# Written lists for the vector work of an up-projection, and earlier reads on the way down

## The chip, the cores and the metric

The kernel runs on one core of one Trainium2 chip. Five engines of the core matter: TensorE (PE, its weight loads shown as PEld), VectorE (DVE), ScalarE (ACT), GpSimd (POOL) and SyncE (SP), which here issues all DMA transfers. Each takes its instructions from a queue of its own, in the order in which the program left them there. The metric is the time of one execution on the device, in microseconds, as the median of the runs shown.

## The reference

One inference step of a two-layer decoder: 1024 tokens of a prompt and 8 x 4 tokens of a sample group share the weights. Each layer has a recurrent mixer, cross attention and a feed-forward part. The change touches the last one:

```python
def conv_ffn(h, w_up, conv_w, conv_b, w_down, prev):
    up = h @ w_up                                   # 1024 -> 2 x 2816
    ext = jnp.concatenate([prev, up], axis=1)
    c = conv_b + conv_w[0] * ext[:, 0:L]
    for j in range(1, CONV_W):                      # CONV_W = 3, causal
        c = c + conv_w[j] * ext[:, j:j + L]
    a, b = jnp.split(c, 2, axis=-1)
    return (silu(a) * b) @ w_down, ext[:, L:]
```

## The kernel before

Every product in float32 is made of three matmuls, `mm3`: both operands are split into a high part (a cast on ScalarE) and a low part (a subtraction on VectorE), and high x high, high x low and low x high are added in a bank of PSUM.

**Units of the up-projection.** `ffn` works through 22 columns f of 128 features, each for both halves (a and b) of `w_up`. Column 0 is done plainly. Each further one, f = 1 to 21, is a *unit*, a product of two 2 x 2 block matrices in the seven products of a Strassen scheme (`products`, L866). A unit has 14 *steps*: products 1, 2, 6, 5, 7, 3, 4 in this order, each for two halves c of 264 columns; a step is 12 matmuls. What a step leaves in its bank is taken by `ffn_take` (L1114) into the tiles `ext`: products 1, 6 and 5 (steps 0, 1, 4, 5, 6, 7) by a copy on ScalarE (L1123), products 2, 7 and 3 (steps 2, 3, 8 to 11) by an add on VectorE (L1127) and a multiplication on GpSimd (L1128), product 4 (steps 12, 13) by a multiplication on VectorE (L1125). Product 6 goes on in the bank of product 1, so step 4 can begin only when the copy of step 0 is done; in the same way steps 8 and 9 follow the copies of steps 4 and 5, steps 10 and 11 those of 6 and 7, and step 12 the add of step 8.

**Weights of the next unit.** `Blocks.steps` (L229) prepares them during the present unit: four sums and differences of 512 columns on GpSimd (L237, L238, L239, L243), and for four sets a cast on ScalarE (L223) and a low part on VectorE (L224). In the trace the sets are `whi`/`wlo` (product 1 and 2), `wh1`/`wl1` (products 5 and 4), `whs`/`wls` (6 and 7, tiles of the same tag) and `w4u` (product 3). Three buffers `wraw` take the raw weights.

**Convolution of the unit before.** `ffn_conv` (L1147) puts its work on the list `slow`: for each half h of the tokens, `first` (two activations, L1169), four `more` (L1172), a silu (L1176) and products (L1186, L1189) that are stored in DRAM; and on GpSimd sums of stored rows (L1199, L1204). `tick` takes items from `slow` as an estimate of free time allows.

**Order.** The tile framework draws the order of every engine's queue: it goes through the program with a model of the instructions' durations and takes from what is ready. So the queues need not have the program's order, and what the model thinks ready may not be so on the chip. `copied` ties the `w4u` parts behind the last copy of `ffn_take`.

**The way down.** `Down.run` (L416) multiplies the stored rows with `w_down` in the same scheme: seven products of six blocks i of 4, 3 and 3 row tiles (48 or 36 matmuls). `load` reads a weight block, `other` a second one where the product takes a sum of two, `sums` adds them on GpSimd, `parts` splits the result (L347), `fetch` reads stored rows y, `join` (L366) subtracts two of them on GpSimd, and `split` (L380) makes their high and low parts.

Of the kernel before, what the change touches and what calls it, by code (L numbers as in the profile page):

```python
# [18 lines left out]
P = 128  # L19
# [4 lines left out]
NS = 8  # L24
# [28 lines left out]
CUTS = ((0, 4), (4, 3), (7, 3))  # L53
OH = 3
# [154 lines left out]
class Blocks:  # L209


    def __init__(self, k, name, srcs, n):
        self.k, self.name, self.srcs, self.n, self.w = k, name, srcs, n, n * P
        self.raw, self.f = [None, None], {}
# [14 lines left out]
    def steps(self, at):  # L229
# [3 lines left out]
        for s in at:  # L233
# [54 lines left out]
class Down:  # L288
# [127 lines left out]
    def run(self):  # L416
# [3 lines left out]
        for i, (p, mp, j) in enumerate(self.at):  # L420
# [8 lines left out]
            for c in range(2):  # L429
# [24 lines left out]
class Kernel:  # L454
    def __init__(self, tc, ins, outs):
# [7 lines left out]
        self.copied = None  # L463
# [52 lines left out]
    def run(self, gen):  # L516
        return Task(gen).finish()

# [347 lines left out]
    def products(self, weights, acts, n, name, take):  # L866
# [4 lines left out]
        for s, (p, c) in enumerate(ORDER):  # L871
# [9 lines left out]
            self.tick(us - take(p, c, ps))  # L881
# [75 lines left out]
    def ffn(self, l, norm, ahead, cuts=None, post=None):  # L957
# [43 lines left out]
        self.ffn_conv(l, 0, exts)  # L1001
        for u, f in enumerate(range(1, NFT)):
            if f % 4 == 1 and f + 3 < NFT:
                state = Task(self.conv_state(l, f + 3))
            exts = self.ffn_ext(l, f)
            for s in self.products(todo[u], acts, 4, f"u{l}_{f}", self.ffn_take(exts, rstd)):
                self.ahead(todo, u, s)
# [12 lines left out]
            self.ffn_conv(l, f, exts)  # L1020
# [126 lines left out]
    def ffn_conv(self, l, f, exts):  # L1147
# [6 lines left out]

        pair, odd = f // 2, f % 2

# [3 lines left out]
        def half(h):  # L1160
            o, w = h * H, (H, CW - H)[h]
            ct = []
            wv = lambda j, q: self.cw[:, j, f + q * NFT:f + q * NFT + 1]

            def first():
                t = self.c(f"ct{l}{f}{h}")
                ct.extend([t[:, (CW - H) * q:(CW - H) * q + w] for q in range(2)] + [t])
                for q in range(2):
                    nc.scalar.activation(out=ct[q], in_=exts[q][0][:, o:o + w], func=AF.Identity, scale=wv(0, q), bias=wv(3, q))  # L1169

            def more(j, q):
                nc.vector.scalar_tensor_tensor(out=ct[q], in0=exts[q][0][:, o + j:o + j + w], scalar=wv(j, q), in1=ct[q], op0=ALU.mult, op1=ALU.add)  # L1172
# [1272 lines left out]
```

## Time and profile before

| | |
|---|---|
| median of three runs | 3252.09 us (3251.09 to 3258.42) |
| the profiled execution, its span | 3257.31 us, 3255.5 us |
| PE, PEld | busy 3110.3 us (96%), 2958.9 us (91%) |
| VectorE, ScalarE, GpSimd | 72%, 43%, 42% busy |
| the chain that ended last | PE 53%, VectorE 24%, GpSimd 12% of the span |
| DMA | 37.5% of 16 engines, mean 123 GB/s |

Busy times are shares of the whole span; a stage can look quite different. A matmul's end is modelled, and matmuls overlap. The chain is followed back from the last instruction to what released each one.

### The profile page before, as it was taken

Reading aid. Unit: us, or ns where it says so; the run is one execution under the profiler, and the core shown is the slowest. Engines: PE = TensorE matmul, PEld = TensorE weight load, DVE = VectorE, ACT = ScalarE, POOL = GpSimd, SP = SyncE. Lnnn points to the kernel's source line nnn. Section 1 sums busy time; section 2 is a strip of 40 time slices with the busy share of each in tenths; the row PEclk is TensorE's granted clock in tenths of the full one; section 3 lists DMA queues with packets and bytes.
Section 4 is the critical chain, followed back from the end, with each engine's and each line's share of the span. In section 5 each row is a group of like instructions: output and inputs, shape, how many; then the busy total and the mean of one; then the engine's idle time right before and its main releaser. Section 6 shows DMA issues by size and latency. Waiting matters only on the chain.

```text
span 3255.5 us, 64230 instructions
## 1 busy us (share of the span) xinstructions
PE 3110.3 (96%) x25741; PEld 2958.9 (91%) x25741; DVE 2329.9 (72%) x4274; ACT 1405.4 (43%) x2788; POOL 1358.7 (42%) x1494
## 2 busy tenths in 40 slices
PE   8999899999989999999999999999999899999988
PEld 6998888998889999999999999889989899999988
DVE  6649967834798787779864444675379977877896
ACT  7222255444464444453342334244446444444424
POOL 4011113300457777736621111240035777774482
PEclk9999999999999999999999999999999999999999
DMA  8513264345122222267531121225422222225853
GB/s 259 193 47 97 82 205 158 106 143 186 44 87 94 87 81 91 94 234 256 184 112 53 45 58 57 81 64 178 147 94 95 82 94 88 79 93 198 282 181 106
DMA packets 391349, 400.05 MB, mean 123 GB/s; under 512 B 26157, under 2 KB 314076, under 8 KB 391052
## 3 DMA queue, kind: packets, MB, share of 16 engines
q1 hardware_dynamic: 391052, 395.97, 37.5%
q8 instruction: 202, 3.31, 0.4%
q14 instruction: 95, 0.78, 0.1%
HBM read 303.84 MB, written 92.05 MB: 122 GB/s over the span
## 4 chain that ended last, share of the span: by engine, by line
PE 53%; DVE 24%; POOL 12%; issue 6%; ACT 3%; DMA 2%; SPq 0%; DVEq 0%; POOLq 0%; ACTq 0%
DVE ct L1172 6%; POOL ext L1128 5%; PE bd L765 3%; PE bd L763 3%; PE bd L764 3%; PE pjxq L764 2%; PE pjxq L763 2%; PE pjxq L765 2%; DVE ct L1186 1%; POOL wru L243 1%; DVE ext L1127 1%; PE blu L763 1%; PE blu L765 1%; ACT ct L1169 1%; PE blu L764 1%
## 5 line engine op out<-in xcount | busy, mean ns | idle before, releaser
L1128 POOL TENSOR_TENSOR ext<-ext,rstdff 128x264 f32<-128x264 f32 (+2 forms) x336 | 327.1, 998 | 187.4 <-DVE ext L1127 186.3
L1172 DVE SCALAR_TENSOR_TENSOR ct<-ext,cw,ct 128x528 f32<-128x528 f32 (+1 forms) x352 | 350.6, 1033 | 65.9 <-ACT ct L1169 65.7
L1169 ACT ACTIVATE ct<-ext,cw 128x544 f32<-128x544 f32 (+1 forms) x176 | 141.1, 831 | 167.8 <-POOL ext L1128 104.4
L763 PE MATMUL blu<-hhff,whiu 128*128 128x264 f32 x672 | 191.6, 286 | 0.0
L765 PE MATMUL blu<-hhff,wlou 128*128 128x264 f32 x672 | 190.8, 285 | 0.0
L892 POOL TENSOR_TENSOR o<-o 128x528 f32<-128x528 f32 x4 | 5.4, 1338 | 359.7 <-DVE xo0bb L273 179.9
L1123 ACT COPY ext<-blu 128x264 f32<-128x264 f32 (+2 forms) x336 | 98.3, 324 | 95.3 <-PE blu L765 95.2
L763 PEld LDWEIGHTS blu<-hhff,whiu 128*128 128x128 f32 x672 | 127.5, 190 | 0.0
L765 PEld LDWEIGHTS blu<-hhff,wlou 128*128 128x128 f32 x672 | 127.2, 189 | 0.0
L764 PE MATMUL pjxq<-hlxa,whxq 128*128 128x352 f32 x384 | 126.3, 329 | 0.0
L763 PE MATMUL pjxq<-hhxa,whxq 128*128 128x352 f32 x384 | 126.2, 329 | 0.0
L765 PE MATMUL pjxq<-hhxa,wlxq 128*128 128x352 f32 x384 | 124.9, 325 | 0.0
L347 DVE TENSOR_TENSOR wlod<-wrd,whid 128x768 fp32r<-128x768 f32 (+1 forms) x60 | 83.3, 1389 | 54.5 <-ACT whid L347 54.5
L347 ACT CAST whid<-wrd 128x768 fp32r<-128x768 f32 (+1 forms) x60 | 54.5, 909 | 151.5 <-PE bd L764 91.4
L1127 DVE TENSOR_TENSOR ext<-ext,blu 128x264 f32<-128x264 f32 (+2 forms) x336 | 107.5, 351 | 0.0
L224 DVE TENSOR_TENSOR w4u<-wru,w4u 128x512 fp32r<-128x512 f32 x42 | 30.3, 721 | 103.9 <-ACT w4u L223 103.9
L763 PE MATMUL blu<-hhff,w4u 128*128 128x264 f32 x336 | 95.8, 285 | 1.1 <-ACT ext L1123 1.1
L764 PE MATMUL blu<-hhff,whiu 128*128 128x264 f32 x336 | 96.7, 288 | 0.0
L764 PE MATMUL blu<-hlff,w4u 128*128 128x264 f32 x336 | 95.6, 285 | 0.0
L765 PE MATMUL blu<-hhff,w4u 128*128 128x264 f32 x336 | 95.5, 284 | 0.0
L764 PE MATMUL blu<-hlff,whiu 128*128 128x264 f32 x336 | 95.5, 284 | 0.0
L1176 ACT ACTIVATE ct<-ct 128x528 f32<-128x528 f32 x88 | 57.4, 652 | 70.7 <-DVE ct L1172 70.7
(2290 smaller groups left out, 12980.4 us busy)
## 6 DMA issues: line engine op xcount, KB each, us to landing
wru<-in_ffn_w_up SPq DMA_DIRECT2D x88, 512.0 KB
wrd<-in_ffn_w_down SPq DMA_DIRECT2D x56, 384.0 KB
bdb<-ct SPq DMA_DIRECT2D x80, 264.0 KB
wrkv<-in_xa_w_kv SPq DMA_DIRECT2D x32, 512.0 KB
kc<-in_cache_mem_k SPq DMA_DIRECT2D x64, 256.0 KB
vc<-in_cache_mem_v SPq DMA_DIRECT2D x64, 256.0 KB
wrd<-in_ffn_w_down SPq DMA_DIRECT2D x28, 512.0 KB
bdt<-ct SPq DMA_DIRECT2D x40, 264.0 KB
```

The source lines that it names most:

```text
L243: gt(out=a[:, w:], in0=a[:, w:], in1=self.s[:, :w], op=ALU.subtract)
L347: self.cast = nc.scalar.copy(out=hi, in_=src), nc.vector.tensor_tensor(out=lo, in0=src, in1=hi, op=ALU.subtract)
L763: nc.tensor.matmul(ps, wh, ah, start=first, stop=False, **kw)
L764: nc.tensor.matmul(ps, wh, al, start=False, stop=False, **kw)
L765: nc.tensor.matmul(ps, wl, ah, start=False, stop=last, **kw)
L1123: self.copied = nc.scalar.copy(out=d, in_=z)
L1127: nc.vector.tensor_tensor(out=d, in0=d, in1=z, op=ALU.add)
L1128: nc.gpsimd.tensor_tensor(out=d, in0=d, in1=r, op=ALU.mult)
L1169: nc.scalar.activation(out=ct[q], in_=exts[q][0][:, o:o + w], func=AF.Identity, scale=wv(0, q), bias=wv(3, q))
L1172: nc.vector.scalar_tensor_tensor(out=ct[q], in0=exts[q][0][:, o + j:o + j + w], scalar=wv(j, q), in1=ct[q], op0=ALU.mult, op1=ALU.add)
L1176: nc.scalar.activation(out=a, in_=a, func=AF.Silu)
L1186: nc.vector.tensor_tensor(out=d[:, :n], in0=a[:, :n], in1=b[:, :n], op=ALU.mult)
```

## The change

The work that `slow` and `Blocks.steps` held during units is cut into named pieces. `UNIT` lists for each step which pieces are issued after the step's bank is taken: `c` is a piece of the convolution of the column before, `w` a piece of the next unit's weights (`d1` to `d4` the differences, `h` a cast, `l` a low part), `s` a sum of rows. From the second unit on, `strict` ties every instruction of these pieces and of `ffn_take`, `ffn_ext` and `ffn_conv` on VectorE, ScalarE and GpSimd to the one before it on its engine, so each queue has the written order. The second raw block of the next but one unit is loaded at step 7, not 13, and the tie `copied` is gone. On the way down rows y are fetched two blocks ahead, not one, and second weight blocks three ahead, not four (six still, from the second product on to the third).

```diff
+ENGINES = (mybir.EngineType.DVE, mybir.EngineType.Activation, mybir.EngineType.Pool)
+UNIT = {0: ("c first 0 1", "c more 0 1 0", "s"), 1: ("c more 0 1 1", "w d3"), 2: ("c more 0 2 0", "w d1"), 3: ("c more 0 2 1", "w d2", "w ha"),
+        4: ("c silu 0", "w la"), 5: ("w h1", "c product 0"), 6: ("w l1", "c first 1 0", "w d4"), 7: ("c first 1 1", "c more 1 1 0"), 8: ("c more 1 1 1",),
+        9: ("c more 1 2 0",), 10: ("w hs", "c more 1 2 1"), 11: ("c silu 1", "w ls"), 12: ("c product 1", "w h4"), 13: ("w l4",)}
 OH = 3
...
@@ -248,10 +254,39 @@
                 self.parts(b, ("s1", "a22"), k.c(f"wh1{n}", F32R)[:, :2 * w], k.c(f"wl1{n}", F32R)[:, :2 * w])
             elif s == 12:
                 t = k.c(f"w4{n}", F32R)
-                with ExitStack() as ctx:
-                    if k.copied is not None:
-                        ctx.enter_context(k.tc.issue_after(k.copied.ins))
-                    self.parts(a[:, w:], ("s4",), t[:, :w], t[:, w:2 * w])
+                self.parts(a[:, w:], ("s4",), t[:, :w], t[:, w:2 * w])
+
+    def piece(self, q):
+
+        k, w, n, nc = self.k, self.w, self.name, self.k.nc
+        gt = nc.gpsimd.tensor_tensor
+        a, b = self.raw
+        if q == "d3":
+            self.s = k.c(f"ws{n}")[:, :2 * w]
+            gt(out=self.s[:, w:], in0=a[:, :w], in1=b[:, :w], op=ALU.subtract)
+        elif q == "d1":
+            gt(out=b[:, :w], in0=b[:, :w], in1=b[:, w:], op=ALU.add)
+        elif q == "d2":
+            gt(out=self.s[:, :w], in0=b[:, :w], in1=a[:, :w], op=ALU.subtract)
+        elif q == "d4":
+            gt(out=a[:, w:], in0=a[:, w:], in1=self.s[:, :w], op=ALU.subtract)
+        elif q[0] == "h":
+            names = {"a": ("a11", "a12"), "1": ("s1", "a22"), "s": ("s2", "s3"), "4": ("s4",)}[q[1]]
+            src = {"a": a, "1": b, "s": self.s, "4": a[:, w:]}[q[1]]
+            if q[1] == "1":
+                t = [k.c(f"{v}{n}", F32R)[:, :2 * w] for v in ("wh1", "wl1")]
+            elif q[1] == "4":
+                t = k.c(f"w4{n}", F32R)
+                t = t[:, :w], t[:, w:2 * w]
+            else:
+                t = [k.wp.tile([P, 1024], F32R, tag=v, name=f"{v}{q[1]}{n}", bufs=2)[:, :2 * w] for v in ("whi", "wlo")]
+            nc.scalar.copy(out=t[0], in_=src)
+            for i, nm in enumerate(names):
+                self.f[nm] = tuple(v[:, i * w:(i + 1) * w].rearrange("p (k c) -> p k c", c=P) for v in t)
+            self.lows[q[1]] = t, src
+        else:
+            t, src = self.lows.pop(q[1])
+            nc.vector.tensor_tensor(out=t[1], in0=src, in1=t[0], op=ALU.subtract)
 
 
 class Group:
...
@@ -438,10 +473,11 @@
                     if i == 0:
                         self.split(0, 4)
                         self.fetch(1, 0)
+                        self.fetch(1, 1)
                     self.parts(i + 1)
                     self.load(i + 3)
-                    self.fetch(*((x + 1, e + 1) if e < np_ - 1 else (x + 2, 0)))
-                    self.other(i + (np_ if DOWN[x] == 2 else 4))
+                    self.fetch(*((x + 1, e + 2) if e < np_ - 2 else (x + 2, e + 2 - np_)))
+                    self.other(i + (np_ if DOWN[x] == 2 else 3))
                     self.join(x + 1, e)
                 else:
...
@@ -515,6 +551,26 @@
 
     def run(self, gen):
         return Task(gen).finish()
+
+    @contextmanager
+    def strict(self):
+
+        bb = self.nc.cur_bb.bb
+        last = bb.instructions[-1]
+        yield
+        if self.order is None:
+            return
+        new = []
+        for i in reversed(bb.instructions):
+            if i is last:
+                break
+            new.append(i)
+        for i in reversed(new):
+            if i.engine in ENGINES:
+                prev = self.order.get(i.engine)
+                if prev is not None:
+                    self.tc.add_manual_dep(i, prev, mybir.DependencyInfo(mybir.DependencyClass.NoSync, mybir.DependencyReason.DATA), reason="order")
+                self.order[i.engine] = i.name
 
 
...
@@ -878,7 +934,9 @@
             for k in range(n):
                 ah, al = (t[:, c * HC:(c + 1) * HC] for t in acts[b][k])
                 self.mm3(ps, wh[:, k], wl[:, k], ah, al, p in STARTS and k == 0, k == n - 1, skip_group_check=p not in STARTS)
-            self.tick(us - take(p, c, ps))
+            with self.strict():
+                spent = take(p, c, ps)
+            self.tick(us - spent)
             yield s
 
...
@@ -999,12 +1057,18 @@
             todo[1].load(q)
         self.tick(1e9)
         self.ffn_conv(l, 0, exts)
+        self.conv["first"](0, 0)
         for u, f in enumerate(range(1, NFT)):
+            self.order = {} if u == 1 else self.order
             if f % 4 == 1 and f + 3 < NFT:
                 state = Task(self.conv_state(l, f + 3))
-            exts = self.ffn_ext(l, f)
+            with self.strict():
+                exts = self.ffn_ext(l, f)
             for s in self.products(todo[u], acts, 4, f"u{l}_{f}", self.ffn_take(exts, rstd)):
-                self.ahead(todo, u, s)
+                if u + 2 < len(todo) and s in (2, 7):
+                    todo[u + 2].load(s == 7)
+                with self.strict():
+                    self.unit_work(f, s, todo[u + 1] if u + 1 < len(todo) else None)
                 if s == 6:
                     if f % 4 == 2 and f + 2 < NFT:
                         state.finish()
@@ -1017,7 +1081,11 @@
                         for k in range(KT):
                             self.dma(self.x[k], self.xd[k])
                 yield
-            self.ffn_conv(l, f, exts)
+            with self.strict():
+                self.ffn_conv(l, f, exts)
+                if f < NFT - 1:
+                    self.conv["first"](0, 0)
+        self.order = None
         last = []
         for i in down.run():
...
@@ -1120,7 +1188,7 @@
             for d, s, v in self.pieces(exts[q], a, HC):
                 z, r = v(ps[:, s]), v(rstd[:, a + s.start:a + s.stop])
                 if p in (1, 6, 5):
-                    self.copied = nc.scalar.copy(out=d, in_=z)
+                    nc.scalar.copy(out=d, in_=z)
                 elif p == 4:
                     nc.vector.tensor_tensor(out=d, in0=z, in1=r, op=ALU.mult)
...
@@ -1151,61 +1219,77 @@
...
+        ct = {}
+        wv = lambda j, q: self.cw[:, j, f + q * NFT:f + q * NFT + 1]
+        def first(h, q):
+            if q == 0:
+                ct[h] = [t[:, (CW - H) * v:(CW - H) * v + w] for v in range(2)] + [t]
+            nc.scalar.activation(out=ct[h][q], in_=exts[q][0][:, o:o + w], func=AF.Identity, scale=wv(0, q), bias=wv(3, q))
+
+        def more(h, j, q):
+            o, w = h * H, (H, CW - H)[h]
+            nc.vector.scalar_tensor_tensor(out=ct[h][q], in0=exts[q][0][:, o + j:o + j + w], scalar=wv(j, q), in1=ct[h][q], op0=ALU.mult, op1=ALU.add)
+
+        def silu(h):
+            nc.scalar.activation(out=ct[h][0], in_=ct[h][0], func=AF.Silu)
+
+        def product(h):
+            a, b, t = ct[h]
+            o = h * H
+            n = min(H, TP - o)
+            if f >= 2 * NPAIR:
+                d, e = b, a[:, :TS]
+            elif h == 0:
+                self.rows[odd] = b, a
+                d = b
+            else:
+                d = self.rows[odd][1]
+                e = d[:, n:H]
+            nc.vector.tensor_tensor(out=d[:, :n], in0=a[:, :n], in1=b[:, :n], op=ALU.mult)
+            if h:
+                js = [t[:, (CW - H) * q + TP + 2 - H:][:, :NS * (LS + 2)].rearrange("p (s j) -> p s j", j=LS + 2)[:, :, :LS] for q in range(2)]
+                nc.vector.tensor_tensor(out=e.rearrange("p (s j) -> p s j", j=LS), in0=js[0], in1=js[1], op=ALU.mult)
+            if f >= 2 * NPAIR:
+                self.dma(self.fd[f][:, o:o + n], d[:, :n])
+                    self.dma(self.fd[f][:, TP:], e)
+            else:
+                store(("b11", "b12", "b21", "b22")[2 * odd + h], d)
+
+        def sums():
+            (a, b), gt = self.rows[0], nc.gpsimd.tensor_tensor
+            if odd:
+                gt(out=b, in0=self.rows[1][1], in1=a, op=ALU.subtract)
+            else:
+                gt(out=a, in0=b, in1=a, op=ALU.subtract)
+            store(("t1", "t2")[odd], (a, b)[odd])
+        self.conv = dict(first=first, more=more, silu=silu, product=product)
+        if f < 2 * NPAIR:
+            self.sums.append((f, sums))
+        if f == NFT - 1:
+            for h in range(2):
+                self.slow += [(0.0, lambda h=h: (first(h, 0), first(h, 1)))] + [(0.65, lambda h=h, j=j, q=q: more(h, j, q)) for j in (1, 2) for q in range(2)]
+                self.slow += [(0.8, lambda h=h: (silu(h), product(h)))]
+
+    def unit_work(self, f, s, nxt):
+
+        for q in UNIT[s]:
+            what, *a = q.split()
+            if what == "w":
+                if nxt is not None:
+                    nxt.piece(*a)
+            elif what == "s":
+                if self.sums and self.sums[0][0] < f - 1:
+                    self.sums.pop(0)[1]()
+            else:
+                self.conv[a[0]](*(int(v) for v in a[1:]))
```

## Rows read from the trace of the kernel before

**Rows 1.** The page's first part: busy time of each engine

```profile
PE 3110.3 (96%) x25741; PEld 2958.9 (91%) x25741; DVE 2329.9 (72%) x4274; ACT 1405.4 (43%) x2788; POOL 1358.7 (42%) x1494
```

**Rows 2.** Windows: length, busy PE, PEld, DVE, ACT, POOL, granted clock, DMA share, GB/s

```profile
957.90:985.00 27.10, 22.94 (x170) 22.52 (x169) 27.10 (x32) 16.78 (x30) 18.51 (x20) 0.87 0.14 40
985.00:1012.40 27.40, 22.68 (x172) 21.62 (x171) 26.47 (x40) 11.52 (x19) 22.51 (x26) 0.97 0.36 112
...
1034.50:1404.30 369.80, 359.21 (x2867) 351.74 (x2866) 290.17 (x435) 167.77 (x306) 286.74 (x358) 1.00 0.27 88
1404.30:1424.90 20.60, 20.60 (x169) 20.40 (x168) 17.41 (x33) 11.36 (x23) 9.24 (x20) 1.00 0.66 218
1425.00:1647.60 222.60, 209.39 (x1683) 207.91 (x1683) 175.58 (x185) 79.25 (x121) 107.31 (x46) 0.98 0.68 227
...
2597.70:2967.40 369.70, 359.18 (x2866) 351.64 (x2866) 290.11 (x435) 167.75 (x306) 286.77 (x358) 1.00 0.28 88
```

**Rows 3.** Waits of PE, 1034.5 to 1404.3: total us, times, longest

```profile
PE blu L763 <- ACT ext L1123: 7.1, 17, 0.4
PE blu L763 <- DVE ext L1127: 3.4, 15, 0.3
```

**Rows 4.** Timeline of PE in step 4 of a unit: start, duration, instruction

```profile
1215.02 0.40 PE L763 MATMUL blu<-ff0t10h,whsu 128*128 128x264 f32 x1 [0.39 <-ACT ext L1123]
...
1215.51 0.28 PE L763 MATMUL blu<-ff0t11h,whsu 128*128 128x264 f32 x1
...
1215.99 0.28 PE L764 MATMUL blu<-ff0t12l,whsu 128*128 128x264 f32 x1
```

**Rows 5.** Timeline of DVE, then ACT, then POOL, in the same unit

```profile
1226.23 0.69 DVE L224 TENSOR_TENSOR w4u<-wru,w4u 128x512 fp32r<-128x512 f32 x1 [2.91 <-ACT w4u L223]
1226.85 0.42 DVE L1127 TENSOR_TENSOR ext<-ext,blu 128x264 f32<-128x264 f32 x1
1227.18 0.76 DVE L1172 SCALAR_TENSOR_TENSOR ct<-ext,cw,ct 128x528 f32<-128x528 f32 x1
...
1213.15 1.56 ACT L1169 ACTIVATE ct<-ext,cw 128x528 f32<-128x528 f32 x2 [1.59 <-DVE ext L1125]
1214.61 0.36 ACT L1123 COPY ext<-blu 128x264 f32<-128x264 f32 x1
...
1222.12 2.19 POOL L1204 TENSOR_TENSOR ct<-ct,ct 128x528 f32<-128x528 f32 x1 [0.18 <-issue]
1224.27 1.28 POOL L243 TENSOR_TENSOR wru<-wru,wsu 128x512 f32<-128x512 f32 x1
```

**Rows 6.** The chain that ended last, in order of time: one activation, two units

```profile
1101.88 0.86 ACT ct L1169
...
1123.63 0.85 ACT ct L1169
```

**Rows 7.** Groups by line and shape, 1034.5 to 1404.3: busy, mean ns, idle before

```profile
L224 DVE TENSOR_TENSOR wlsu<-wsu,whsu 128x1024 fp32r<-128x1024 f32 x18 | 29.2, 1620 | 0.0
...
L243 POOL TENSOR_TENSOR wru<-wru,wsu 128x512 f32<-128x512 f32 x17 | 21.8, 1284 | 0.0
...
L224 DVE TENSOR_TENSOR w4u<-wru,w4u 128x512 fp32r<-128x512 f32 x17 | 11.8, 693 | 51.3 <-ACT w4u L223 51.3
```

**Rows 8.** Timeline of DVE and POOL early in that unit

```profile
1211.59 1.17 DVE L1172 SCALAR_TENSOR_TENSOR ct<-ext,cw,ct 128x544 f32<-128x544 f32 x1 [1.66 <-ACT ct L1169]
...
1210.90 1.29 POOL L237 TENSOR_TENSOR wsu<-wru,wru 128x512 f32<-128x512 f32 x1
1212.26 1.66 POOL L238 TENSOR_TENSOR wru<-wru 128x512 f32<-128x512 f32 x1
```

**Rows 9.** Timeline of DVE in unit 2: the last products of unit 1

```profile
995.87 0.76 DVE L1125 TENSOR_TENSOR ext<-blu,rstdff 128x264 f32<-128x264 f32 x2
```

**Rows 10.** Waits of POOL on the way down of layer 0

```profile
POOL yrt3b L366 <- DMA yrt3b<-bdb: 5.4, 4, 3.3
```

**Rows 11.** Waits of PE on the way down of layer 0

```profile
PE bd L765 <- DVE wlod L347: 12.6, 6, 3.9
```

More of the change, by code (lines that the diff above doesn't have):

```diff
@@ L1 @@
 import math
-from contextlib import ExitStack
+from contextlib import ExitStack, contextmanager
 import numpy as np
@@ L213, in __init__ @@
         self.k, self.name, self.srcs, self.n, self.w = k, name, srcs, n, n * P
-        self.raw, self.f = [None, None], {}
+        self.raw, self.f, self.lows = [None, None], {}, {}
     def load(self, q):
@@ L462, in __init__ @@
         self.pending, self.held = None, []
-        self.copied = None
+        self.order = None
         self.vcol = {}
@@ L1019, in ffn @@
                 yield
-            self.ffn_conv(l, f, exts)
+            with self.strict():
+                self.ffn_conv(l, f, exts)
+                if f < NFT - 1:
+                    self.conv["first"](0, 0)
+        self.order = None
         last = []
@@ L1155, in ffn_conv @@
         pair, odd = f // 2, f % 2
+        ct = {}
+        wv = lambda j, q: self.cw[:, j, f + q * NFT:f + q * NFT + 1]
         def store(nm, t):
             self.dma(self.bd[nm][pair // 2][pair % 2], t)
-        def half(h):
+        def first(h, q):
             o, w = h * H, (H, CW - H)[h]
-            ct = []
-            wv = lambda j, q: self.cw[:, j, f + q * NFT:f + q * NFT + 1]
-            def first():
+            if q == 0:
                 t = self.c(f"ct{l}{f}{h}")
[L1167 to L1172, printed above, removed]
-            def product():
-                a, b, t = ct
-                nc.scalar.activation(out=a, in_=a, func=AF.Silu)
-                n = min(H, TP - o)
-                if f >= 2 * NPAIR:
-                    d, e = b, a[:, :TS]
-                elif h == 0:
-                    self.rows[odd] = b, a
-                    d = b
-                else:
-                    d = self.rows[odd][1]
-                    e = d[:, n:H]
-                nc.vector.tensor_tensor(out=d[:, :n], in0=a[:, :n], in1=b[:, :n], op=ALU.mult)
-                if h:
-                    js = [t[:, (CW - H) * q + TP + 2 - H:][:, :NS * (LS + 2)].rearrange("p (s j) -> p s j", j=LS + 2)[:, :, :LS] for q in range(2)]
-                    nc.vector.tensor_tensor(out=e.rearrange("p (s j) -> p s j", j=LS), in0=js[0], in1=js[1], op=ALU.mult)
-                if f >= 2 * NPAIR:
-                    self.dma(self.fd[f][:, o:o + n], d[:, :n])
-                    if h:
-                        self.dma(self.fd[f][:, TP:], e)
-                else:
-                    store(("b11", "b12", "b21", "b22")[2 * odd + h], d)
-            return [(0.0, first)] + [(0.65, lambda j=j, q=q: more(j, q)) for j in (1, 2) for q in range(2)] + [(0.8, product)]
@@ L1197, in first_sum @@
-        def first_sum():
-            a, b = self.rows[0]
-            gt(out=a, in0=b, in1=a, op=ALU.subtract)
-            store("t1", a)
-        def second_sum():
-            (a, b), d = self.rows[0], self.rows[1][1]
-            gt(out=b, in0=d, in1=a, op=ALU.subtract)
-            store("t2", b)
-        gt = nc.gpsimd.tensor_tensor
-        self.slow += self.sums + half(0) + half(1)
-        self.sums = [(0.0, second_sum if odd else first_sum)] if f < 2 * NPAIR else []
+                ct[h] = [t[:, (CW - H) * v:(CW - H) * v + w] for v in range(2)] + [t]
```

## The prediction

> **What bounds the kernel now.** I read the page first, then a table of windows by stage, then who waits for whom on PE, then the timeline of the three other engines around one wait.
>
> On the page PE is busy 96% of the span [rows 1]: whatever the change gives must come out of PE's gaps. The windows say where they lie [rows 2]. Units 4 to 20 of the first layer's up-projection last 369.8 us for 17 units, 21.75 us each (the second layer: 369.7). Unit 21, which prepares no weights for a next one, has as many matmuls (168 and a neighbour) in 20.60 us, and PE is busy in all of it. So a unit loses about 1.15 us. Units 1 and 2 take 27.1 and 27.4 us, with a granted clock of 0.87 and 0.97 (a mix of the two levels). The way down takes 222.6 us with PE busy for 209.4.
>
> A regular unit loses it at two places [rows 3, 4]: once before the first matmul of step 4 (it waits for a ScalarE copy, 7.1 us in 17 waits) and once before that of step 12 (for a VectorE add, 3.4 us in 15 waits). These sum to 0.62 us a unit, not 1.15, because a matmul is booked with 0.28 us while four of them start in 0.48 us [rows 4]: a gap shows only what is longer than that overlap.
>
> By the Trainium skill (Perfetto Trace Analysis, "Identifying the Most-Contended Engine") matmul busy time is a poor measure of room on TensorE and the weight loads' busy time a good one. The trace agrees: weight loads fill 351.74 of 369.8 us, so 18.1 us are open, 1.06 a unit; by PE's busy time 10.6 us, 0.62 a unit. By the one the two layers' regular units have about 38 us to give, by the other 22.
>
> Why the two are late is in the queues [rows 5]. Step 4 needs the copy of step 0's bank. It stood at 1214.61, three steps after its bank was full, behind two conv activations (1213.15) that had waited for VectorE's last product of the unit before. Step 12 needs the add of step 8's bank. On VectorE it stood (1226.85) behind w4u's low part (1226.23, 2.91 us idle for ScalarE's cast), the cast behind GpSimd's difference (1224.27), and that behind a sum of 2.19 us (1222.12). No engine is full; each instruction stands behind one that waits elsewhere. The chain that ended last shows it from the other side [rows 6]: it comes back to the same activation after 21.75 us by way of VectorE, GpSimd and ScalarE alone. That loop, not PE, sets the unit.
>
> **The change part by part.** No instruction of the up-projection is removed; durations stay, order changes.
>
> *The lists, units 2 to 21.* Step 0's copy now stands ahead of the activations of its own step, so it runs as soon as its bank is full, three steps (3 x 20.6/14 = 4.4 us) before step 4 asks. In front of step 8's add on VectorE stand, from the end of step 3 on, the add of step 3, one conv term, the low part `la`, a product, `l1` and another term. At their contended durations this is 0.42 + 1.17 + 1.62 + 0.69 + 1.62 + 1.17 = 6.7 us (the product taken like w4u's part, which is about as wide) [rows 5, 7, 8]. Step 12 begins eight steps, 11.8 us, after the end of step 3: with the add itself there is room of 4.6 us for what these wait for ScalarE on the way. `w4u` no longer stands in that way: it comes at steps 12 and 13 and is asked for at step 10 of the next unit. Both waits should go. What is next late: VectorE itself. It is busy 290.17/17 = 17.1 us a unit and GpSimd 16.9; in 20.5 us that is 83% for each, so the lists can hold if they run dry for less than 3.4 us a unit.
>
> Price: a unit without the waits lies between 20.2 us (168 x 0.12) [rows 4] and unit 21's 20.6 [rows 2]; I take 20.5, near the row of a whole unit. Units 3 to 20 give 18 x 1.25 = 22.5 us, unit 21 0.1: 22.6 us a layer, 45.2 in all.
>
> *The port.* VectorE and GpSimd hinder each other: a conv term takes 0.76 us at its shortest here and 1.17 us when GpSimd is in a 512-column difference; it ends 0.57 us after that difference ended (1210.90 + 1.29), and GpSimd's next (1212.26) ends 1.16 us after it [rows 5, 8]. So the parts that exclude each other are about 0.57 of 0.76 and 1.16 of 1.28. Per unit VectorE's two-input work, uncontended, is 8 x 0.76 for the terms, 1.38 x 3 + 0.69 for the low parts (twice w4u's for twice its width) and some 1.4 for the products: 12.3 us. GpSimd's is 4 x 512 + 528 + 1584 columns at the 1.28 us per 512 of its differences [rows 7], 10.4 us. The parts held are 0.75 x 12.3 + 0.91 x 10.4 = 18.7 us, under 20.5.
>
> The Trainium skill (SBUF — State Buffer, "Who interferes with whom") says the pair of ports is held for the whole instruction. By that a unit needs 12.3 + 10.4 = 22.7 us and can't run in 20.5; 36 regular units would come out 34 us slower than now, at 3286. The trace has the exclusion but not its full length: the same work runs in 21.75 now.
>
> *Units 1 and 2.* Unit 1 is not chained. VectorE is busy in 53.6 of 54.5 us, and unit 1's last products come out from 995.87 on, some 11 us after PE ended that unit (985.0) [rows 2, 9]. Order makes no work vanish: what PE gains is only how far VectorE may trail it at the end. Against it, ScalarE's strict queue blocks at step 0's activation, which needs that product, and step 1's copy stands behind. I bound it at 5 us a layer either way (three steps of trailing more, or the same as a stall) and take 1.5 gained: 3.0 in all.
>
> *The way down.* Each y block is read one block (4.4 to 5.8 us) sooner. GpSimd's joins now wait 5.4 us for such reads in layer 0 [rows 10], so at most some 11 us in two layers. PE's own waits are for VectorE's `wlod` (12.6 us, six waits) [rows 11], whose queue is full and stretched by GpSimd: sooner joins move that, they don't remove it. Against it, second blocks are asked for three blocks ahead rather than four. Two of these that come a short block (36 matmuls, 4.4 us) late would cost 9. More tiles are open as well, and SyncE's queue waits where a tile is not free. I take 4 us gained, bounds 9 lost and 11 gained.
>
> *The rest.* `w4u` loses its tie to the last copy, nothing behind it. Loads of the next but one unit go at step 7, not 13: earlier than needed, hidden by a whole unit. The stores of products and sums leave SyncE with their producers, up to half a unit later than now; their reader is the way down, and the last pair's rows have a unit's time.
>
> Sum: 45.2 + 3 + 4 = 52 us off the profiled execution's 3257.3, that is 3205. This execution lay 5.2 us above the median of the runs, 3252.1; by the median 3200 us.
>
> **The rivals.**
> *One wait stays or a new one takes its place.* For it: a strict queue has a head. ScalarE's `ha` needs a buffer that is free only when step 3 ends, and behind it stand the copy of step 4's bank (asked for at step 8) and silu 0, for which VectorE's product 0 and all behind that wait; `hs` stands so behind step 9, with silu 1 and `h4` behind it; GpSimd's sum waits for product 1, and the multiplies and differences stand behind that sum. Against: none of the things held up is asked for within three steps. If half of the loss stays, the regular units give 23 and the rest 7: 3222.
> *An idle head binds: slower.* With the port held for 18.7 us, a unit may leave it idle for 21.75 - 18.7 = 3.0 us before it lasts longer than now. VectorE's wait for w4u is now 51.3/17 = 3.0 us a unit [rows 7]. If the lists keep a wait of that size at another head and add half a step (0.74 us), a unit takes 18.7 + 3.7 = 22.4 us, and 36 units cost 23 us more: 3275. Against: the lists spread VectorE's work to 0.7 to 2.2 us in each step of 1.47, so no head has to wait long.
> *The port held for whole instructions: slower.* The uncontended sum of 22.7 us binds as soon as the order no longer lets VectorE's one-input adds run beside GpSimd: 3286, as above. Against: the present unit is shorter than that sum. The rule beside it is that of the Trainium skill (SBUF — State Buffer, "Who interferes with whom").
> *The order was no cause.* If PE's waits come from unit 2's lag that never heals, units stay at 21.75: 3245 with the rest. Against: the chain closes within one unit [rows 6].
> *More than forecast.* Units of 20.2 (36 x 0.3 = 11 us more), 5 a layer from units 1 and 2 and 11 from the way down: 45 + 11 + 10 + 11 = 77, 3175.
>
> **How the numbers follow.** Forecast 0.64; one wait stays 0.18; an idle head 0.07; whole instructions 0.02; order no cause 0.04; more 0.05. The forecast's own range is 3187 to 3212 (20.3 to 20.6 a unit is 8 less and 4 more, the start and the way down the rest). To 2 in 10 left out: 3184 to 3226, which takes in the rival of half the loss and leaves out the slow side. Within 0.2% (6.5 us, what a measurement of this kernel can tell from no change) 0.06, faster 0.85, slower 0.09 (the two slower rivals).
>
> **What will show it.** Right: 20.4 to 20.6 us a unit from unit 4 on, no PE wait for the copy L1123 or the add L1127 in them, ScalarE's copy of step 0 within a microsecond of step 0's end, the chain back on PE in those stretches, and w4u's wait on VectorE gone. Wrong: a PE wait at one step in every unit, or VectorE and GpSimd together without a pause at 21 us or more (then the port binds). Units 1 and 2 above 55 us together would show the backlog step wrong; the way down above 225 us the reads.

## The result, and the profile after

The changed kernel takes 3203.89 us (median of four runs, 3203.51 to 3210.28), the kernel before 3254.10 beside it: a ratio of 0.9849, 95% interval 0.9832 to 0.9867. Forecast were 3200 and a range of 3184 to 3226. The profiled execution took 3210.28 us, its span is 3208.3, that of before 3255.5: 47.2 us less, in these stages (a unit is measured from its first matmul to the next unit's; us, first layer / second layer):

| stage | before | after | gain, both layers | forecast |
|---|---|---|---|---|
| units 1 and 2 | 54.5 / 54.3 | 50.6 / 50.8 | 7.4 | 3.0 |
| units 3 to 20, each | 21.77 / 21.78 | 20.53 / 20.58 | 43.9 | 45.0 |
| unit 21 | 20.6 / 20.7 | 20.3 / 20.4 | 0.6 | 0.2 |
| way down | 222.6 / 223.5 | 223.1 / 224.5 | -1.5 | 4 |
| end of the first way down to unit 1 of the second layer | 873.4 | 877.3 | -3.9 | 0 |

Of the 0.7 us that are missing to the 47.2, 0.2 lies ahead of the first unit and 0.3 behind the last way down; the rest is rounding and the joints of the stages.

The page's busy line and the windows of the changed kernel (length, then busy PE, PEld, DVE, ACT, POOL, granted clock, DMA share, GB/s) for unit 1, unit 2, units 4 to 20, unit 21, the way down, and units 4 to 20 of the second layer:

```profile
PE 3091.1 (96%) x25741; PEld 2953.9 (92%) x25741; DVE 2363.6 (74%) x4274; ACT 1410.4 (44%) x2788; POOL 1406.9 (44%) x1494
```

```profile
957.70:985.00 27.30, 23.14 (x171) 22.71 (x170) 27.30 (x32) 16.78 (x29) 18.71 (x18) 0.87 0.16 46
985.00:1008.30 23.30, 21.49 (x172) 20.84 (x171) 21.85 (x34) 10.52 (x20) 20.74 (x25) 1.00 0.33 107
...
1028.70:1377.90 349.20, 349.20 (x2868) 348.99 (x2867) 310.59 (x438) 171.75 (x307) 309.50 (x361) 1.00 0.29 93
1377.90:1398.20 20.30, 20.30 (x170) 20.30 (x169) 16.73 (x28) 11.74 (x23) 9.69 (x15) 1.00 0.81 266
1398.30:1621.40 223.10, 212.66 (x1684) 211.05 (x1683) 180.10 (x190) 78.84 (x121) 108.09 (x52) 0.97 0.68 228
...
2570.00:2919.90 349.90, 349.90 (x2867) 349.69 (x2866) 311.04 (x438) 171.78 (x307) 309.52 (x360) 1.00 0.29 93
```

Against [rows 2], PE and its weight loads now fill units 4 to 20 from end to end: no wait of PE is left in them. VectorE and GpSimd are busy for 310.6 and 309.5 us there, where it was 290.2 and 286.7 in a stretch 20.6 us longer: the same instructions take longer in sum, which fits their meeting more often (below, VectorE's product of 528 columns takes 1.80 us where 0.69 was priced). Unit 12, which starts at 1192.9, in the timeline, first DVE, then ACT, then POOL (start, duration, instruction, idle before):

```profile
1193.45 0.72 DVE L289 TENSOR_TENSOR w4u<-wru_12False,w4u 128x512 fp32r<-128x512 f32 x1
...
1200.84 1.67 DVE L289 TENSOR_TENSOR wloau<-wru_13False,whiau 128x1024 fp32r<-128x1024 f32 x1
1202.44 1.80 DVE L1255 TENSOR_TENSOR ct<-ct 128x528 f32<-128x528 f32 x1
1204.16 2.31 DVE L289 TENSOR_TENSOR wl1u<-wru_13True,wh1u 128x1024 fp32r<-128x1024 f32 x1
...
1207.29 0.42 DVE L1195 TENSOR_TENSOR ext<-ext,blu 128x264 f32<-128x264 f32 x1
...
1194.63 0.38 ACT L1191 COPY ext<-blu 128x264 f32<-128x264 f32 x1 [3.81 <-PE blu L821]
...
1194.20 1.84 POOL L1271 TENSOR_TENSOR ct<-ct 128x528 f32<-128x528 f32 x1
...
1203.75 1.64 POOL L272 TENSOR_TENSOR wru_13False<-wru_13False,wsu 128x512 f32<-128x512 f32 x1
```

Step 0 ends at 1194.4 and ScalarE's copy of it starts at 1194.63; in [rows 5] it came three steps late. The low part of `w4u` waits for nothing, where VectorE stood 2.91 us before it. The chain in this stretch, by line, is PE alone, in place of the loop of [rows 6]:

```profile
by line: PE blu L821 33.3%; PE blu L820 33.2%; PE blu L819 33.2%; PE cops L1008 0.2%; PE csps L997 0.2%
```

### The profile page after: what moved, and what is told of

It is laid out like the page before. It is cut to its first block, busy times and chain, and to the rows that moved or that the text cites. A ratio compares the mean times of both kernels' runs of the same rounds, so it can differ in the third digit from the quotient of the medians.

```text
span 3208.3 us, 64288 instructions
## 1 busy us (share of the span) xinstructions
PE 3091.1 (96%) x25741; PEld 2953.9 (92%) x25741; DVE 2363.6 (74%) x4274; ACT 1410.4 (44%) x2788; POOL 1406.9 (44%) x1494
## 4 chain that ended last, share of the span: by engine, by line
PE 72%; DVE 16%; issue 4%; POOL 3%; DMA 2%; ACT 2%; SPq 0%; DVEq 0%; POOLq 0%; ACTq 0%
PE blu L819 8%; PE blu L821 8%; PE blu L820 8%; PE bd L821 2%; PE bd L819 2%; PE bd L820 2%; PE pjxq L820 2%; PE pjxq L819 2%; PE pjxq L821 2%; DVE wlod L382 1%; DVE s5sc L2390 1%; DMA wrd<-in_ffn_w_down 1%; DVE hlff L135 1%; DVE hlxa L135 1%; PE kcp L1535 1%
## 5 line engine op out<-in xcount | busy, mean ns | idle before, releaser
L1196 POOL TENSOR_TENSOR ext<-ext,rstdff 128x264 f32<-128x264 f32 (+2 forms) x336 | 332.4, 1010 | 104.4 <-DVE ext L1195 103.6
L1238 DVE SCALAR_TENSOR_TENSOR ct<-ext,cw,ct 128x528 f32<-128x528 f32 (+1 forms) x352 | 322.1, 920 | 33.4 <-ACT ct L1234 33.3
L819 PE MATMUL blu<-hhff,whiau 128*128 128x264 f32 x640 | 182.8, 286 | 0.0
L821 PE MATMUL blu<-hhff,wloau 128*128 128x264 f32 x640 | 182.1, 285 | 0.0
L819 PEld LDWEIGHTS blu<-hhff,whiau 128*128 128x128 f32 x640 | 121.4, 190 | 0.0
L821 PEld LDWEIGHTS blu<-hhff,wloau 128*128 128x128 f32 x640 | 120.7, 189 | 0.0
L1255 DVE TENSOR_TENSOR ct<-ct 128x528 f32<-128x528 f32 x88 | 103.5, 1177 | 0.0
L820 PE MATMUL blu<-hhff,whiau 128*128 128x264 f32 x320 | 91.9, 287 | 0.0
L820 PE MATMUL blu<-hlff,whiau 128*128 128x264 f32 x320 | 91.0, 284 | 0.0
L1671 POOL TENSOR_TENSOR khg<-khg,tothg 128x512 f32<-128x512 f32 (+1 forms) x24 | 33.0, 1377 | 122.8 <-PE shg L1642 57.0
```

The source lines that it names most:

```text
L819: nc.tensor.matmul(ps, wh, ah, start=first, stop=False, **kw)
L820: nc.tensor.matmul(ps, wh, al, start=False, stop=False, **kw)
L821: nc.tensor.matmul(ps, wl, ah, start=False, stop=last, **kw)
L1196: nc.gpsimd.tensor_tensor(out=d, in0=d, in1=r, op=ALU.mult)
L1238: nc.vector.scalar_tensor_tensor(out=ct[h][q], in0=exts[q][0][:, o + j:o + j + w], scalar=wv(j, q), in1=ct[h][q], op0=ALU.mult, op1=ALU.add)
L1255: nc.vector.tensor_tensor(out=d[:, :n], in0=a[:, :n], in1=b[:, :n], op=ALU.mult)
```

## The experiments

Twelve kernels beside the change. Each ratio is to the kernel before, run on the same chip. The earlier load of the second raw block (step 7, not 13) is in all of them but reads_alone; it was not run apart.

| run | us | ratio, 95% interval | units 3 to 20, each |
|---|---|---|---|
| the change | 3203.9 | 0.9849 (0.9832 to 0.9867) | 20.53 / 20.58 |
| no_ties | 3292.9 | 1.0124 (1.0110 to 1.0138) | 22.98 / 23.08 |
| vec_only | 3210.4 | 0.9865 (0.9851 to 0.9880) | 20.73 / 20.72 |
| act_pool_only | 3224.3 | 0.9907 (0.9890 to 0.9924) | 21.17 / 21.18 |
| ties_from_unit1 | 3202.4 | 0.9840 (0.9827 to 0.9854) | 20.53 / 20.54 |
| head_back | 3234.7 | 0.9937 (0.9922 to 0.9952) | 21.31 / 21.32 |
| head_back_mended | 3230.6 | 0.9931 (0.9912 to 0.9951) | 21.27 / 21.25 |
| head_back_plus1 | 3288.1 | 1.0105 (1.0090 to 1.0120) | 22.97 / 22.99 |
| plus1 | 3214.9 | 0.9881 (0.9866 to 0.9896) | 20.71 / 20.75 |
| pool_plus2 | 3263.2 | 1.0029 (1.0019 to 1.0039) | 21.96 / 22.02 |
| reads_alone | 3254.3 | 1.0004 (0.9995 to 1.0012) | 21.77 / 21.80 |
| lists_alone | 3200.1 | 0.9838 (0.9825 to 0.9852) | 20.53 / 20.56 |
| unit1_old_reads | 3199.8 | 0.9834 (0.9820 to 0.9849) | 20.53 / 20.56 |

**Which order.** Four runs take ties away or add them.

```diff
 # no_ties: strict() ends after its yield
-        if self.order is None:
-            return
+        return
 # vec_only
-ENGINES = (mybir.EngineType.DVE, mybir.EngineType.Activation, mybir.EngineType.Pool)
+ENGINES = (mybir.EngineType.DVE,)
 # act_pool_only
+ENGINES = (mybir.EngineType.Activation, mybir.EngineType.Pool)
 # ties_from_unit1
-            self.order = {} if u == 1 else self.order
+            self.order = {} if u == 0 else self.order
```

> The changed kernel without the ties: the pieces stand in the program in the order of the lists, and the framework draws the order of the queues. If the tied order is what removed PE's waits, they come back for the most part: 21 to 21.75 us a regular unit, 3222 to 3250 in all, with a wait of PE in every unit for ScalarE's copy or VectorE's add. The rival: the place of the pieces in the program is enough, units stay at 20.5 and the time within 0.2% of the changed kernel's 3204.

> The changed kernel with the ties on VectorE alone; ScalarE's and GpSimd's queues are the framework's. Without any tie a unit took 20.5 to 25.4 us, and VectorE stood 2.9 us before w4u's low part with five adds behind it. If VectorE's order is the one that counts, its add of step 8 no longer stands behind w4u, PE's wait at step 12 goes and units take 20.5 to 20.8 us: 3204 to 3216. If the loop through the three engines counts (GpSimd's sum ahead of the difference, ScalarE's cast behind it), VectorE's tied queue waits for casts that come late, and a unit stays above 21 us: 3225 to 3290.

> The changed kernel with the ties on ScalarE and GpSimd, and VectorE's queue the framework's. If VectorE's order is the one that counts, PE waits again at step 12 for its add and a unit takes 21 us or more: 3225 to 3290. If it is enough that casts and differences come in time, nothing on VectorE is late whatever stands ahead of it, and the time stays within 0.3% of 3204.

> The changed kernel with the ties from the first unit on, not the second. If the order of the queues is what unit 1 loses by, units 1 and 2 fall from 50.6 and 50.8 us to some 46 to 48, and the time to 3195 to 3200. The rival is the prediction's: VectorE is full from end to end of unit 1 (27.3 of 27.3 us), order makes no work vanish, and units 1 and 2 stay within 1 us of 50.6, the time within 0.1% of 3204. A third: the strict queues add stalls to the backlog, and it is 2 to 8 us slower.

Without ties the kernel is not half way back but 40 us slower than before. PE's waits of 1033 to 1401 (total us, times, longest), and DVE, ACT, POOL and PE in unit 12, which starts at 1217.3:

```profile
PE blu L818 <- DVE ext L1194: 19.0, 10, 2.5
PE blu L818 <- ACT ext L1190: 6.0, 11, 2.0
```

```profile
1233.04 1.49 DVE L289 TENSOR_TENSOR w4u<-wru_13False,w4u 128x512 fp32r<-128x512 f32 x1 [2.93 <-ACT w4u L283]
1234.45 3.47 DVE L1237 SCALAR_TENSOR_TENSOR ct<-ext,cw,ct 128x528 f32<-128x528 f32 x2
1237.85 1.16 DVE L1194 TENSOR_TENSOR ext<-ext,blu 128x264 f32<-128x264 f32 x4
...
1232.39 0.62 ACT L283 CAST w4u<-wru_13False 128x512 fp32r<-128x512 f32 x1 [3.62 <-POOL wru_13False L272]
...
1228.91 2.20 POOL L1268 TENSOR_TENSOR ct<-ct,ct 128x528 f32<-128x528 f32 x1 [0.18 <-ACT ext L1190]
1231.07 1.28 POOL L272 TENSOR_TENSOR wru_13False<-wru_13False,wsu 128x512 f32<-128x512 f32 x1
...
1238.32 0.59 PE L818 MATMUL blu<-ff0t10h,wh1u 128*128 128x264 f32 x1 [2.46 <-DVE ext L1194]
```

It is the jam of [rows 5] again, and deeper: sum, difference, cast, low part, and behind the low part here two conv terms too, before VectorE comes to four adds at once. Step 12 waits 2.46 us for the first of them. The pieces' place in the program is thus worth nothing by itself; the tied order makes 89 us of difference.

With VectorE alone tied, steady units take 20.5 us (units 5 to 20 show no wait of PE; units 3 and 4, at 22.4 and 22.2, carry most of the excess). With the other two tied and VectorE free, most units keep one wait from unit 7 on, before step 12, the longest 0.3 us in this window of units 4 to 20, and steady units take 21.0 us:

```profile
PE blu L819 <- DVE ext L1195: 3.2, 12, 0.3
```

So it is VectorE's order that counts most, as the first reading of each of these two expectations had it (act_pool_only came 0.7 us below its range of 3225 to 3290). The two gains do not add: VectorE's ties alone give 44 us, the other two queues' alone 30, all three 50.

Either kind of tie alone ends the wait at step 4: act_pool_only shows none for a copy in its window, where step 0's copy stands first. In vec_only it goes too, though there step 0's copy still stands behind an activation that waits for VectorE's product of the unit before. Unit 12 there, DVE and ACT; step 4 begins at 1199.90, without a wait:

```profile
1195.34 0.42 DVE L1193 TENSOR_TENSOR ext<-blu,rstdff 128x264 f32<-128x264 f32 x1
...
1195.79 0.83 ACT L1234 ACTIVATE ct<-ext,cw 128x528 f32<-128x528 f32 x1 [5.43 <-DVE ext L1193]
...
1197.81 0.66 ACT L1191 COPY ext<-blu 128x264 f32<-128x264 f32 x2
```

The product starts 4.6 us ahead of step 4 here; in the unit of [rows 5] it started 2.3 us ahead (at 1212.69, step 4 at 1215.02). No run puts the activations ahead of the copy back with all else as in the change.

Ties from the first unit on make unit 1 longer (27.3 to 28.3 us) and unit 2 shorter (23.3 to 21.9); together they stay within 0.4 us, the prediction's rival.

**The place of one head, and its lateness.** A head is the instruction at which a queue stands and waits. `w4u`'s pieces go back in front of the add of step 8.

```diff
 # head_back_mended; head_back has "s" in entry 6, before "w d4"
-        0: ("c first 0 1", "c more 0 1 0", "s")
+        0: ("c first 0 1", "c more 0 1 0")
-        4: ("c silu 0", "w la")
+        4: ("c silu 0", "w la", "s")
-        7: ("c first 1 1", "c more 1 1 0")
+        7: ("c first 1 1", "c more 1 1 0", "w h4", "w l4")
-        12: ("c product 1", "w h4"), 13: ("w l4",)
+        12: ("c product 1",), 13: ()
 # head_back_plus1: as head_back, and
-        6: ("w l1", "c first 1 0", "s", "w d4")
+        6: ("w l1", "c first 1 0", "s", "w d2", "w d4")
```

> The changed kernel, all ties kept, with w4u's head of before put back: GpSimd's sum stands at step 6 just ahead of the difference that makes w4u, the cast and the low part come at step 7, so VectorE's add of step 8 stands behind the low part. Worked out from the changed kernel's unit 12 (it starts at 1192.9): the sum would run from 1203.8 to 1206.0, the difference to 1207.4, the cast to 1208.1, the low part to 1208.8 and the add to 1209.2, and step 12 starts at 1210.5. If lateness and not the place is what costs, PE waits for nothing and the time stays within 0.2% of 3204. The rival, by which the place behind a low part that waits for a cast is itself the loss: PE waits at step 12 in each unit, 20.8 to 21.2 us a unit, 3215 to 3228.

> As the run with w4u's head put back, and GpSimd's second difference of 512 columns (128 x 512, 1.3 to 1.6 us) is computed once more, to the same values, between the sum and w4u's difference. By the same working the add of step 8 now ends at 1210.5 to 1210.8, when step 12 starts. If lateness costs, this dose is where the wait begins: PE waits 0 to 0.5 us at step 12 in every unit for VectorE's add, 20.5 to 21.1 us a unit, 3204 to 3226, and in each unit VectorE idles before w4u's low part. The rival that only the load of GpSimd and VectorE counts: the extra work is 1.2 us of the pair of ports, 18.7 + 1.2 = 19.9 us of 20.5, no wait and 3204.

> The run with w4u's head put back once more, but with the sum named at step 4, before that step's product 0 replaces the rows it reads. The run before named it at step 6, where in every second unit it took rows of the pair then under way; GpSimd has nothing else to do in steps 4 and 5, so its queue is the same. If those rows had no part in the time: 21.3 us a unit, 3230 to 3236, VectorE idle for 1.8 us before w4u's low part and PE waiting at step 12 for the add. If the sum had waited for the product, units are shorter, 20.5 to 21, 3204 to 3222.

head_back and head_back_plus1 leave out the order between the sum and the product that replaces its rows, so in every second unit they sum rows of the pair under way; head_back_mended keeps it. The first expectation was wrong and its rival nearly right: 21.3 us a unit, and from unit 4 on PE waits at step 12; the time came 7 us above the rival's range. The second took too little by 60 us. The third came out as its first reading had it, 21.3 us and 3230.6. In head_back_mended, unit 12 (start 1198.6), DVE, POOL, ACT, PE:

```profile
1215.66 0.69 DVE L289 TENSOR_TENSOR w4u<-wru_13False,w4u 128x512 fp32r<-128x512 f32 x1 [1.84 <-ACT w4u L283]
1216.27 0.42 DVE L1195 TENSOR_TENSOR ext<-ext,blu 128x264 f32<-128x264 f32 x1
...
1210.91 2.33 POOL L1271 TENSOR_TENSOR ct<-ct 128x528 f32<-128x528 f32 x1
1213.20 1.78 POOL L272 TENSOR_TENSOR wru_13False<-wru_13False,wsu 128x512 f32<-128x512 f32 x1
...
1215.01 0.62 ACT L283 CAST w4u<-wru_13False 128x512 fp32r<-128x512 f32 x1 [3.25 <-POOL wru_13False L272]
...
1216.75 0.39 PE L819 MATMUL blu<-ff0t10h,wh1u 128*128 128x264 f32 x1 [0.39 <-DVE ext L1195]
```

The add starts 17.7 us after its unit does; in the changed kernel (above) it starts 14.4 us after. My working had put it at 15.9: it kept the starts of the undisturbed unit. But the late add makes GpSimd's multiplications of this unit late, and these the differences of the next: the first starts 3.9 us after its unit does, in the changed kernel 3.1. So the lateness settles higher than one unit shows. That fits the first units of head_back_mended in layer 0, where units 4 to 6 still show no wait and take 20.5 us and the wait sets in with unit 7.

With one more difference in the same queue PE waits longer by about its length. Waits of PE in 1030 to 1378 in head_back, then in head_back_plus1 (total us, times, longest):

```profile
PE blu L819 <- DVE ext L1195: 6.4, 15, 0.5
```

```profile
PE blu L819 <- DVE ext L1195: 25.5, 16, 3.4
```

That is 1.2 us more a wait, where the differences of [rows 7] take 1.28. The wait is 3.4 us in the first of these units and between 0.6 and 2.2 us in the others. A unit takes 23.0 us there on the mean, and part of this is the clock (last section). head_back and head_back_mended differ by less than their intervals, so in head_back the rows that the sum read have no part in the time; head_back_plus1 was not run with its sum at step 4.

**How full the pair is.** VectorE and GpSimd are loaded with one or two doses: the same extra difference where nothing that PE asks for stands behind it:

```diff
 # plus1
-        6: ("w l1", "c first 1 0", "w d4")
+        6: ("w l1", "c first 1 0", "w d2", "w d4")
 # pool_plus2
-        4: ("c silu 0", "w la")
+        4: ("c silu 0", "w la", "w d2")
-        8: ("c more 1 1 1",)
+        8: ("c more 1 1 1", "w d2")
```

> The changed kernel, all ties and places kept, and GpSimd's second difference of 512 columns computed once more, to the same values, ahead of w4u's difference at step 6. With w4u's head ahead of the add of step 8 the same extra difference took a unit from 21.3 to 23.0 us. If what costs is lateness ahead of an instruction that PE asks for, nothing is asked for behind this one: no wait of PE, 20.5 us a unit, within 0.2% of 3204. By the sum of the ports it is 18.7 + 1.2 = 19.9 us of 20.5, which holds too. The rival: GpSimd, busy for 18.2 us a unit and stretched by the shared ports, has no room left, and units take 20.8 to 21.5 us: 3214 to 3240.

> As the run with one more difference, but two, at steps 4 and 8. By the prediction's sum of the ports 18.7 + 2 x 1.2 = 21.1 us, over the 20.5 us of a unit: the ports (or GpSimd, 18.2 + 2.6 = 20.8 us) become the bound, a unit takes 20.8 to 21.5 us, 36 units cost 11 to 36 us, 3215 to 3240, and GpSimd and VectorE have no idle time left. The rival: the exclusion is weaker than the sum takes it, and units stay at 20.5 to 20.6, 3204 to 3208. The other: waits chain up as where w4u's head stood ahead of the add, above 22 us a unit, 3260 or more.

The same window of 1060 to 1360 in the changed kernel, in plus1 and in pool_plus2:

```profile
1060.00:1360.00 300.00, 300.00 (x2464) 299.79 (x2464) 264.73 (x376) 148.18 (x264) 264.12 (x312) 1.00 0.29 93
```

```profile
1060.00:1360.00 300.00, 300.00 (x2444) 298.07 (x2443) 291.87 (x368) 144.41 (x260) 297.65 (x315) 1.00 0.29 92
```

```profile
1060.00:1360.00 300.00, 287.87 (x2305) 281.95 (x2305) 290.74 (x345) 133.19 (x247) 297.81 (x314) 1.00 0.27 88
```

One difference more and GpSimd is busy 99% and VectorE 97% of the time; no wait of PE shows, but a unit takes 20.71 us and plus1 is 11 us slower than the change, at the lower edge of its rival. The second difference costs its full length, 21.96 - 20.71 = 1.25 us a unit, more than the forecast of pool_plus2 had. The time, 3263, lies in the range of its last reading, but not for that reason: no wait of GpSimd shows, and the chain runs back on it, through its multiplications (L1196, 32.8%) and differences (L270, 23.5%). From one dose to two GpSimd, stretched by VectorE, is the bound. If the first dose needs as much as the second, then without any dose it needs 20.71 - 1.25 = 19.5 us of a unit of 20.5; this is an estimate. A dose on VectorE alone, which would tell the pair of ports from GpSimd's own queue, was not run. The same difference, put ahead of the add of step 8, had cost 1.7 us a unit (head_back to head_back_plus1), here 0.2: here the place cost more than the load.

**The reads.** One run has them alone, two take them out.

```diff
 # lists_alone, unit1_old_reads; reads_alone is the kernel before with the + and - changed over
-                        self.fetch(1, 1)
-                    self.fetch(*((x + 1, e + 2) if e < np_ - 2 else (x + 2, e + 2 - np_)))
-                    self.other(i + (np_ if DOWN[x] == 2 else 3))
+                    self.fetch(*((x + 1, e + 1) if e < np_ - 1 else (x + 2, 0)))
+                    self.other(i + (np_ if DOWN[x] == 2 else 4))
```

> The kernel before with only the reads on the way down changed: rows two blocks ahead, second weight blocks three ahead. By the prediction's sum 4 us faster than before, so a ratio of 0.999; by the rival (the reads are hidden in either order) within 0.05% of before, and the way down within 1 us of 222.6 and 223.5. In both the regular units stay at 21.75 us.

> The changed kernel with the way down as before: rows fetched one block ahead, second weight blocks asked for four ahead. By the prediction's sum the reads give 4 us, so this run comes out at the changed kernel's 3204 + 4 = 3208 and the way down at 223 to 225 us a layer. The rival, from the two traces, in which the way down lasts 223.1 and 224.5 us with the new reads and 222.6 and 223.5 without: the reads cost about 1 us in all or nothing, and this run is 3200 to 3204. In both, regular units stay at 20.5 us.

> The changed kernel with ties from the first unit on and the way down's reads as before. If the two small gains add (the old reads gave 3.8 us in the medians, the ties of unit 1 gave 1.5), 3198 to 3201, a ratio of 0.983 to 0.984 to the kernel before. The rival: both lie inside what single runs differ by, and it comes out at 3200 to 3204.

The prediction's 4 us show in neither run. The reads alone change nothing that can be measured (way down 222.6 and 223.8 us), and a gain of 4 us, a ratio of 0.9988, lies outside the interval; lists_alone came out where its rival had it (3200, not 3208). Taking them out made the way down 221.2 and 222.4 us in the profile, but the medians' intervals overlap with that of the change, and unit1_old_reads, with the same way down, shows 222.9 and 222.3: it comes out level with lists_alone and the best of all, by less than the intervals tell. Waits on the way down of layer 0 in reads_alone:

```profile
ACT whid L347 <- POOL wrd L336: 35.7, 8, 9.8
...
PE bd L766 <- DVE wlod L347: 7.9, 6, 2.5
...
PE bd L764 <- ACT whid L347: 4.0, 1, 4.0
...
POOL yrt3b L366 <- DMA yrt3b<-bdb: 3.4, 1, 3.4
```

Against [rows 10, 11] the joins wait less for their reads (5.4 to 3.4 us) and PE less for `wlod` (12.6 to 7.9), but PE has a new wait of 4.0 us for a cast. ScalarE's casts now wait 35.7 us for sums of second blocks (10.8 before). That fits blocks asked for one block later; the two edits were not run apart.

## Why the prediction was right

**The sum.** In the profiled executions 47.2 us were gained where 52 were forecast. The regular units, which are nearly all of it, missed by 1.1. That the sum came so near is in part luck: units 1 and 2 gave 4.4 us more than their term, the way down 5.5 less.

**The regular units** were forecast at 20.5 us and came at 20.53 and 20.58; the loop that the chain showed before was the cause, since its pieces return with the waits when the ties go (no_ties) and one of its links alone, the one before step 12, brings 0.7 us a unit back (head_back_mended). The link before step 4 was not put back alone; its wait goes with VectorE's ties as with those of the other two. Of the two measures of PE's room, the open time of the weight loads (1.06 us a unit) was the nearer one, as the Trainium skill's rule (Perfetto Trace Analysis, "Identifying the Most-Contended Engine") had it; the gain was 1.2.

**The room before step 12** was taken as 4.6 us and is about 2.8: the add ends at 1207.71, step 12 begins at 1210.5. The product was priced at 0.69 us and took 1.80, `l1` at 1.62 and took 2.31: with `la` before them they are three two-input instructions in a row on VectorE, and they run beside GpSimd's differences of 1201.39 and 1203.75. It was room enough.

**The port** was summed to 18.7 us a unit; the two doses put the need at an estimated 19.5. By that the margin was 1.0 us, not 1.8, and the forecast stood on it. The sum left out GpSimd's copies of a few columns (L1093, L1152, L1153), 19.9 us in units 4 to 20 before, 1.2 a unit. One of the three, before and then in the changed kernel (L1161):

```profile
L1093 POOL COPY ext<-cst 128x16 f32<-128x16 f32 x34 | 6.5, 200 | 0.0
```

```profile
L1161 POOL COPY ext<-cst 128x16 f32<-128x16 f32 x34 | 15.6, 468 | 0.0
```

So these are held up as well; whether they are the missing 0.8 us no run shows. The rival of whole instructions, as it was priced (22.7 us a unit), is refuted by the 20.5. The rule beside it, from the Trainium skill (SBUF — State Buffer, "SBUF: two separate sides"), has the one that starts first hold the pair for the whole instruction. The traces agree on the exclusion; by the durations that the profile books it was shorter, 0.57 of 0.76 us and 1.16 of 1.28 [rows 5, 8]. Part of that lies in the booking: on VectorE alone a low part of 0.69 us is followed by the next instruction 0.62 us after its start [rows 5], so booked durations add up to more than an engine needs.

**A wait that stays, an idle head**: neither came. But head_back_plus1 shows that the second could have come: with one head put back and one difference more the time is 3288.

**Units 1 and 2** gave 7.4 us where 3.0 were taken, inside the bound of 5 a layer. The term counted only the backlog that VectorE brings from unit 1, and for that it held (ties_from_unit1). It left out that unit 2 loses by the order of its queues as well: PE waited there 2.7 us for an add and 1.8 for copies, now 0.9 and 0.5, and the granted clock of that unit went from 0.97 to 1.00.

**The way down** was forecast at 4 us gained; nothing was gained, inside the bounds of 9 lost and 11 gained. The step that failed is the side on which I put it: the waits of reads_alone look as if sooner joins and later second blocks cancel, but that is argued, since the two edits were not run apart.

**The stretch between the layers**, 3.9 us longer in this execution, lasts 871.2 to 877.3 us in the profiles of all these kernels, so it is no cost of the change. It may be part of why the profiled execution lies 6.4 us above the median.

## What to carry to other kernels

When no engine is full and PE still waits, look for an instruction that stands behind one that waits for a third engine, and ask of each queue what may stand ahead of what PE asks for. Tie that queue first (here VectorE's, which gave 44 of 50 us); the same order in the program without a tie was 40 us worse than the old order. Before adding work to such a list, measure with a dose how full it is: busy shares of 89% looked like 2.3 us of room in 20.5, and by the doses it was about 1.0.

## What I had not expected

The clock adds to a late queue. In no_ties the wait of 2.46 us in unit 12 is followed by matmuls that start 0.22 us apart, where it is 0.12 in a full unit:

```profile
1238.71 0.42 PE L819 MATMUL blu<-ff0t10l,wh1u 128*128 128x264 f32 x1
1238.93 0.42 PE L820 MATMUL blu<-ff0t10h,wl1u 128*128 128x264 f32 x1
```

The windows of that unit and the next (columns as above):

```profile
1217.30:1242.70 25.40, 22.57 (x171) 22.13 (x170) 18.58 (x27) 10.07 (x19) 17.29 (x28) 0.93 0.25 80
1242.70:1263.20 20.50, 20.50 (x170) 20.50 (x169) 15.91 (x25) 9.42 (x18) 12.72 (x16) 1.00 0.28 92
```

The granted clock of the first is 0.93, a mix of the levels of 2.4 and 1.2 GHz, and it lasts 25.4 us; the next lasts 20.5 at 1.00. In head_back_plus1 a unit with a wait of 1.95 us (1216.4 to 1240.7) has 0.93 as well. Where PE's waits in a unit are 0.3 to 0.5 us (head_back_mended) or up to 1.0 (pool_plus2), it stays at 1.00 in the window of 1060 to 1360. No such stretch is left in units 3 to 21 of the changed kernel.
